# Weights and conditioning loads in separate rings: a two-layer decoder trunk with adaLN

## The chip, the cores and the metric

One Trainium2 chip, one core of it, one program launch. The engines of the core run side by side, each its own queue of instructions: TensorE (PE) with its weight loads (PEld), VectorE (DVE), ScalarE (ACT), GpSimd (POOL), and SyncE (SP), which here only issues transfers from HBM. The metric is the device time of one execution in microseconds; lower is better.

## The reference

Everything is float32; one sequence of 256 positions, model width 1024, two layers.

```python
def ada_mod(c, w, b):
    m = jax.nn.silu(c) @ w + b            # c: (1, 1024), w: (1024, 6144)
    return jnp.split(m[:, None, :], 6, axis=-1)

for layer in range(2):
    shift_m, scale_m, gate_m, shift_f, scale_f, gate_f = ada_mod(c, ada_w[layer], ada_b[layer])
    h = rms_norm(x, norm_gains[layer, 0]) * (1 + scale_m) + shift_m
    y = attn_hybrid_mixer(h, ...) if layer == 0 else retention_mixer(h, ...)
    x = x + gate_m * y
    h = rms_norm(x, norm_gains[layer, 1]) * (1 + scale_f) + shift_f
    gt, up = jnp.split(h @ w_gate_up, 2, axis=-1)       # 2 x 2816 columns
    x = x + gate_f * ((jax.nn.silu(gt) * up) @ w_down)
return rms_norm(x, final_norm)
```

The attention of layer 0 (8 stick-breaking heads, 8 block-sparse heads with rotary) and the retention of layer 1 (4 heads) are small beside the projections: q/k/v 1024x3072, o 1024x1024, retention 1024x6144 and 2048x1024. The six vectors of a layer are one product of a single row with a 1024x6144 matrix, 25 MB a layer, and are all that uses `ada_w`.

## The kernel before, in words

**Weight units.** A float32 product is made of three products of halves: every operand is split into a high part `h` (a copy in the reduced type `float32r`) and a low part `l` (the rest), and `wh*hh`, `wl*hh` and `wh*hl` (lines 422, 423, 426) add up in one PSUM tile. A weight unit is 512 KB, two blocks of 128 rows by 512 columns. SP loads it into a tile `raw`; ACT writes its `wh` (line 220), DVE its `wl` (line 221), each in two pieces of 128x512; then each of the two token tiles (t = 0 and 1, 128 positions each) takes 6 matmuls from it, so 12 in all. There are 228 units: q/k/v 24 (the first 12 in an opening loop of its own over the 8 blocks `kb` of the contraction), o 8, gate-up of layer 0 44, down 22, retention 48 and 16, gate-up of layer 1 44, down 22. The marks `gu0`, `dn0`, `ret`, `gu1`, `dn1` are the numbers of a stage's first unit.

**Buffers.** `raw` is a ring of `NRAW` = 4 tiles (`rawp`), which grows by ten homes during the feed-forward stages, when tiles of the attention stand idle (`raw_homes(True)`). The pairs `wh`/`wl` are a ring of `WBUFS` = 8. Token tile 0 leads token tile 1 by 3 units up to the o projection and by 5 after it (`LAGS`); a pair is held until tile 1 has used it.

**adaLN.** `ada_w` comes in 96 blocks of 512 KB. The 16 blocks of (layer 0, vectors 0 and 1) go through PE in the opening (`ada0_*`). The other 80 go through `ada_unit`: SP loads a block into the same ring `raw`, and DVE multiplies it by its column of silu(c) and adds it to a sum (line 339, `aacc`). `spread` says at which weight unit a block is loaded and summed, ahead of the unit's own load and split. After the eighth block a task turns the sum into columns (`ada_mod`: line 369, a copy on ACT at line 373, then line 379) or a gate (`ada_gate`: ACT line 352, DVE line 353, PE lines 357 and 358). A task's `yield n` lets n ticks of the matmul loop pass; a unit has two ticks for each token tile.

**Order.** PE runs in the order of the program text. ACT, DVE, POOL and SP are put in order when the program is built, by a scheduler that goes by when an instruction can start and by a priority; only instructions that are "pinned" (`tc.keep_in_program_order`, or `pin` while `strict` is set) keep the order of the text among themselves. `more` prepares units `AHEAD` of the one that token tile 0 is at, as far as pairs are free.

**Opening.** For each token: two sums of squares on ACT (line 226), their root (lines 245 to 251), the scaled token (line 255), its transposes on PE (line 953), and a copy by ACT (`xnT`, line 954); with the scale and shift of line 931 and 933 that gives a block of h (DVE line 942, ACT `hh` line 944, DVE `hl` line 947). The first three units' weights come in halves (line 965), and `first_split` splits them. `warm_up` is n matmuls on a tile of zeros.

## Time and profile before

| | |
|---|---|
| median of 3 runs | 771.63 us (769.98, 771.63, 772.52) |
| the profiled execution | 772.73 us, its span 770.9 us |
| PE, PEld busy | 733.2 us (95%), 583.7 us (76%) |
| DVE, ACT, POOL busy | 558.4 us (72%), 405.0 us (53%), 57.1 us (7%) |
| HBM read | 173.16 MB, mean 227 GB/s over the span |

The span runs from the first to the last instruction, and 1.8 us lie around it. PE is the busiest engine: of the profile's 40 slices it is under 9 tenths in the first, the last and five between (116 to 173, 347 to 366 and 501 to 520 us). DVE, at 72% over the whole span, is at 9 tenths or more in eight slices between 77 and 308 us.

### The profile page before, as it was taken

Reading aid. Unit: us, or ns where it says so; the run is one execution under the profiler, and the core shown is the slowest. Engines: PE = TensorE matmul, PEld = TensorE weight load, DVE = VectorE, ACT = ScalarE, POOL = GpSimd, SP = SyncE. Lnnn points to the kernel's source line nnn. Section 1 sums busy time; section 2 is a strip of 40 time slices with the busy share of each in tenths; the row PEclk is TensorE's granted clock in tenths of the full one; section 3 lists DMA queues with packets and bytes.
Section 4 is the critical chain, followed back from the end, with each engine's and each line's share of the span. In section 5 each row is a group of like instructions: output and inputs, shape, how many; then the busy total and the mean of one; then the engine's idle time right before and its main releaser. Section 6 shows DMA issues by size and latency. Waiting matters only on the chain.

```text
span 770.9 us, 10529 instructions
## 1 busy us (share of the span) xinstructions
PE 733.2 (95%) x3564; PEld 583.7 (76%) x3564; DVE 558.4 (72%) x960; ACT 405.0 (53%) x836; POOL 57.1 (7%) x137
## 2 busy tenths in 40 slices
PE   5999998889999999998999999989999999999996
PEld 2777775667888788787787878767877888888884
DVE  3667998779999599647867768676588666665553
ACT  5348645875655455535545454454575455555531
POOL 1001000110000100010111211202110000000000
PEclk9999999999999999999999999999999999999998
DMA  9977888667999879627564747666847787655301
GB/s 306 364 254 244 278 286 292 194 229 252 369 353 333 290 268 393 241 82 217 180 216 142 222 145 226 217 211 201 281 146 214 224 238 211 209 182 180 127 1 54
DMA packets 114806, 174.91 MB, mean 227 GB/s; under 512 B 7496, under 2 KB 71184, under 8 KB 114752
## 3 DMA queue, kind: packets, MB, share of 16 engines
q1 hardware_dynamic: 113376, 171.86, 68.7%
q10 hardware_dynamic: 816, 1.60, 0.6%
q0 software_dynamic: 560, 0.77, 0.3%
q8 instruction: 28, 0.46, 0.3%
q14 instruction: 26, 0.21, 0.1%
HBM read 173.16 MB, written 1.05 MB: 226 GB/s over the span
## 4 chain that ended last, share of the span: by engine, by line
PE 71%; DMA 10%; DVE 8%; ACT 4%; issue 3%; POOL 2%; SPq 0%; DVEq 0%; ACTq 0%; POOLq 0%
PE acc L422 22%; PE acc L426 22%; PE acc L423 21%; DMA raw<-in_ada_w_dram 5%; DVE wl L221 3%; DMA raw<-in_att_w_qkv_dram 2%; DMA raw<-in_att_w_o_dram 2%; ACT wh L220 2%; DVE aacc L339 1%; PE pt L795 1%; DMA early<-in_ada_w_dram 1%; DMA raw<-in_ffn_w_gate_up_dram 1%; PE pt L916 1%; POOL v L248 1%; ACT w L286 1%
## 5 line engine op out<-in xcount | busy, mean ns | idle before, releaser
L221 DVE TENSOR_TENSOR wl<-raw,wh 128x512 fp32r<-128x512 f32 x456 | 297.6, 686 | 123.5 <-ACT wh L220 121.1
L220 ACT ACTIVATE wh<-raw 128x512 fp32r<-128x512 f32 x456 | 265.3, 624 | 208.7 <-PE acc L426 101.4
L422 PE MATMUL acc<-wh,hh 128*128 128x512 f32 x640 | 258.7, 404 | 8.6 <-ACT hh L944 6.8
L423 PE MATMUL acc<-wl,hh 128*128 128x512 f32 x640 | 251.0, 392 | 0.0
L426 PE MATMUL acc<-wh,hl 128*128 128x512 f32 x640 | 205.4, 396 | 0.8 <-DVE hl L290 0.8
L422 PEld LDWEIGHTS acc<-wh,hh 128*128 128x128 f32 x640 | 120.9, 189 | 36.6 <-ACT hh L944 7.6
L426 PEld LDWEIGHTS acc<-wh,hl 128*128 128x128 f32 x640 | 119.6, 189 | 27.8 <-DVE hl L290 2.0
L423 PEld LDWEIGHTS acc<-wl,hh 128*128 128x128 f32 x640 | 121.2, 189 | 23.3 <-issue 0.2
L339 DVE SCALAR_TENSOR_TENSOR aacc<-raw,sc,aacc 128x1024 f32<-128x1024 f32 x80 | 102.4, 1279 | 18.4 <-DMA raw<-in_ada_w_dram 17.2
L422 PE MATMUL acc<-wh,act 128*128 128x512 f32 x240 | 94.1, 392 | 0.0
L423 PE MATMUL acc<-wl,act 128*128 128x512 f32 x240 | 93.5, 389 | 0.0
L426 PE MATMUL acc<-wh,act 128*128 128x512 f32 x240 | 74.3, 391 | 0.0
L422 PEld LDWEIGHTS acc<-wh,act 128*128 128x128 f32 x240 | 45.1, 188 | 10.0 <-ACT wh L220 0.8
L423 PEld LDWEIGHTS acc<-wl,act 128*128 128x128 f32 x240 | 45.1, 188 | 9.2
L426 PEld LDWEIGHTS acc<-wh,act 128*128 128x128 f32 x240 | 44.8, 188 | 9.2
L784 ACT ACTIVATE w<-acc 128x256 f32<-128x256 f32 x44 | 16.9, 384 | 28.7 <-PE acc L426 28.7
L785 DVE TENSOR_TENSOR w<-w,acc 128x256 f32<-128x256 f32 x44 | 18.3, 416 | 9.9 <-ACT w L784 9.7
L226 ACT ACTIVATE w<-x 128x512 f32<-128x512 f32 x20 | 12.5, 623 | 19.1 <-DVE x L308 18.3
L334 POOL MEMSET aacc<- 128x1024 f32 x10 | 9.4, 960 | 176.9 <-PE pt L369 86.7
L229 POOL TENSOR_SCALAR ss<-ss 128x1 f32<-128x1 f32 x8 | 2.4, 303 | 266.8 <-ACT w L226 266.8
L740 ACT ACTIVATE w<-w,ry 128x512 f32<-128x512 f32 x8 | 5.8, 724 | 30.3 <-POOL ry L215 30.3
L306 DVE TENSOR_TENSOR w<-acc,gate 128x512 f32<-128x512 f32 x16 | 11.0, 687 | 13.0 <-PE acc L426 13.0
(165 smaller groups left out, 606.3 us busy)
## 6 DMA issues: line engine op xcount, KB each, us to landing
raw<-in_ffn_w_gate_up_dram SPq DMA_DIRECT2D x176, 256.0 KB, 4.5
raw<-in_ada_w_dram SPq DMA_DIRECT2D x80, 512.0 KB, 5.3
raw<-in_ffn_w_down_dram SPq DMA_DIRECT2D x44, 512.0 KB, 4.3
raw<-in_ret_w_in_dram SPq DMA_DIRECT2D x32, 512.0 KB, 4.3
raw<-in_att_w_qkv_dram SPq DMA_DIRECT2D x21, 512.0 KB, 6.2
early<-in_ada_w_dram SPq DMA_DIRECT2D x16, 512.0 KB, 8.6
raw<-in_ret_w_in_dram SPq DMA_DIRECT2D x32, 256.0 KB, 3.9
raw<-in_ret_w_o_dram SPq DMA_DIRECT2D x16, 512.0 KB, 4.7
```

What stands on the lines that cost most here:

```text
L220: pin(nc.scalar.activation(hi, src, AF.Copy))
L221: pin(nc.vector.tensor_tensor(lo, src, hi, op=ALU.subtract))
L226: pin(nc.scalar.activation(w2(t), xt[t][:, half * 512:(half + 1) * 512], AF.Square, scale=1.0 / 32.0, accum_out=ss))
L248: pin(g.tensor_scalar(v, s1, s0, None, op0=ALU.add))
L306: nc.vector.tensor_mul(m, ps, gate[:, half * 512:(half + 1) * 512])
L334: nc.gpsimd.memset(a, 0.0)
L339: nc.vector.scalar_tensor_tensor(a, r, sc[:, kk:kk + 1], a, op0=ALU.mult, op1=ALU.add)
L422: nc.tensor.matmul(ps, hi[:, kb, :], a, start=first, stop=False)
L423: nc.tensor.matmul(ps, hi[:, kb, :], b, start=False, stop=False)
L426: nc.tensor.matmul(ps, lo[:, kb, :], wh[:, j * 512:(j + 1) * 512], start=False, stop=last)
L784: nc.scalar.activation(s[:, :256], ps[:, :256], AF.Silu)
L785: nc.vector.tensor_mul(s[:, :256], s[:, :256], ps[:, 256:])
```

## The change

The ring `raw` is left to the weights alone, with three tiles instead of four, and the adaLN blocks get a ring of their own, `ada`, of three. `ada_load` issues a block's load; its sum (`ada_unit`) is written two units later (`LATER`, `step`, `due`), or earlier if three are due, and is pinned on DVE. Weights are loaded `DEPTH` units ahead of their split (`load_upto`): two, or five in the feed-forward stages. The pairs `wh`/`wl` go from 8 to 7. The gate's sum is made in the gate's own tile. In the tasks, `GW` goes from 6 to 12 ticks and the two waits of `ada_mod` from 4 and 3 to 6 and 6.

Of the first gate (layer 0, vector 2) six of eight blocks are loaded in the opening, at `kb` 4 to 7, together with the first three units of the attention stage; the 18 blocks left of 24 are spread over units `first` to `gu0` - 6 instead of `first` + 4 to `gu0` - 4. During the opening, raw tiles also live in the attention's `prob` and `sps` tiles.

In the opening's text, the columns and warm-up now stand inside token 0's start, token 0's transposes behind the scale and shift of block 0, and token 1's whole start behind the first splits of all three units; two more matmuls on zeros stand ahead of token 1's transposes.

```diff
@@ -37,15 +37,17 @@
 GY = 4
 R0, R1, R2 = 6, 4, 14
 QR, QP = 6, 3
-GW = 6
+GW = 12
 PRIO = 600
-WBUFS = 8
+WBUFS = 7
 NPS = 8
-NRAW = 4
+NRAW, NADA = 3, 3
+DEPTH = (2, 5)
+LATER = 2
 WIDE = 2
 CONSTS = 4
 EARLY = 2
-WARM = (5, 1)
+WARM = (5, 1, 2)
 
 
 @with_exitstack
@@ -59,7 +61,7 @@
     nc = tc.nc
 
     cp = ctx.enter_context(tc.tile_pool(name="cp", bufs=1))
-    rawp = ctx.enter_context(tc.tile_pool(name="rawp", bufs=NRAW))
+    rawp = ctx.enter_context(tc.tile_pool(name="rawp", bufs=1))
     whp = ctx.enter_context(tc.tile_pool(name="whp", bufs=WBUFS))
     hp = ctx.enter_context(tc.tile_pool(name="hp", bufs=1))
     ap = ctx.enter_context(tc.tile_pool(name="ap", bufs=1))
@@ -320,23 +322,41 @@
         homes.append(homes.pop(0))
         return pool.tile([P, 1024], F32, tag=tag, name=nm("raw"), bufs=bufs)
 
-    def raw_homes(wide):
-
-        homes[:] = [(rawp, "raw", NRAW)] * NRAW
-        if wide:
-            homes.extend([(hp, "oqh", 1), (hp, "oql", 1), (wp, "prob", 2), (wp, "sps", 2),
-                          (wp, "prob", 2), (wp, "sps", 2)])
-
-    def ada_unit(l, m, kk):
+    def raw_homes(*more):
+
+        homes[:] = [(rawp, "raw", NRAW)] * NRAW + list(more)
+
+    due = []
+    now = [0]
+
+    def ada_load(l, m, kk):
+        if len(due) == NADA:
+            ada_sums(1)
+        r = rawp.tile([P, D], F32, tag="ada", name=nm("raw"), bufs=NADA)
+        nc.sync.dma_start(r, ada_w[l, kk * P:(kk + 1) * P, m * D:(m + 1) * D])
+        due.append((now[0], (l, m, kk, r)))
+
+    def ada_sums(n):
+
+        for _ in range(n):
+            ada_unit(*due.pop(0)[1])
+
+    def step():
+        now[0] += 1
+        ada_sums(sum(at + LATER <= now[0] for at, _ in due))
+
+    def ada_unit(l, m, kk, r):
         if kk == 0:
-            a = wp.tile([P, D], F32, tag="aacc", name=nm("aacc"), bufs=2)
+            if m in (2, 5):
+                a = cp.tile([P, D], F32, tag="gate", name=nm("gate"), bufs=1)
+            else:
+                a = wp.tile([P, D], F32, tag="aacc", name=nm("aacc"), bufs=2)
             ada_acc[l, m] = a
             nc.gpsimd.memset(a, 0.0)
             nc.gpsimd.dma_start(a[0:1, :], ada_b[l:l + 1, m * D:(m + 1) * D])
         a = ada_acc[l, m]
-        r = raw_tile()
-        nc.sync.dma_start(r, ada_w[l, kk * P:(kk + 1) * P, m * D:(m + 1) * D])
-        nc.vector.scalar_tensor_tensor(a, r, sc[:, kk:kk + 1], a, op0=ALU.mult, op1=ALU.add)
+        tc.keep_in_program_order(nc.vector.scalar_tensor_tensor(
+            a, r, sc[:, kk:kk + 1], a, op0=ALU.mult, op1=ALU.add))
         if kk == KD - 1:
             if m in (2, 5):
                 spawn(ada_gate(l, m))
@@ -344,8 +364,7 @@
                 spawn(ada_mod(l, m - 1))
 
     def ada_gate(l, m):
-        a = ada_acc.pop((l, m))
-        g = cp.tile([P, D], F32, tag="gate", name=nm("gate"), bufs=1)
+        a = g = ada_acc.pop((l, m))
         for i in range(2):
             c = slice(i * 512, (i + 1) * 512)
             hi, lo = (wp.tile([P, 512], F32R, tag="w2", name=nm("gh"), bufs=2) for _ in range(2))
@@ -362,7 +381,7 @@
 
     def ada_mod(l, m):
         accs = [ada_acc.pop((l, m)), ada_acc.pop((l, m + 1))]
-        yield 4
+        yield 6
         yield ("ps", 1, 1)
         p = pt()
         for g in range(4):
@@ -372,7 +391,7 @@
         r = w2()
         nc.scalar.activation(r, p, AF.Copy)
         release(1)
-        yield 3
+        yield 6
         yield ("ps", 1, 1)
         p = pt()
         for j in range(4):
@@ -394,9 +413,9 @@
 
     def load(i):
         if i == marks["gu0"] + WIDE or i == marks["gu1"] + WIDE:
-            raw_homes(True)
+            raw_homes((hp, "oqh", 1), (hp, "oql", 1), *idle)
         elif i == marks["ret"]:
-            raw_homes(False)
+            raw_homes()
         src, _ = units[i]
         raw = raw_tile().rearrange("p (k f) -> p k f", k=2)
         if isinstance(src, list):
@@ -934,7 +953,7 @@
 
     def ada0_block(kb, rr, ts=(0, 1)):
         k1 = slice(kb, kb + 1)
-        if 0 in ts:
+        if rr is not None:
             ada0_mods(kb, rr)
         hs = {}
         for t in ts:
@@ -958,7 +977,8 @@
         pin(scaled(xns[t][i], xt[t][:, i * 512:(i + 1) * 512], rstd[t]))
 
     NP = KD // 2
-    raw_homes(False)
+    idle = [(wp, tag, 2) for _ in range(2) for tag in ("prob", "sps")]
+    raw_homes(*idle)
     raws = [raw_tile() for g in range(3)]
     for j in range(2):
         for g in range(3):
@@ -971,6 +991,9 @@
     def token_start(t):
         for i in range(2):
             square(t, i)
+        if t == 0:
+            columns()
+            warm_up(WARM[1])
         rstd.append(rms_rstd(t, nc.vector))
         xns.append([w2(t), w2(t)])
         xnT.append(wp.tile([P, KD, P], F32, tag="aacc", name=nm("xnT"), bufs=2))
@@ -984,17 +1007,16 @@
     strict[0] = True
     log_table()
     token_start(0)
-    columns()
-    warm_up(WARM[1])
-    xn_T(0, 0)
     rr = ada0_sum(rows.pop(0))
     gain_columns()
     ws = [w_tiles() for g in range(3)]
     first_split(0, 0)
-    token_start(1)
-    ada0_block(0, rr, (0,))
+    ada0_mods(0, rr)
+    xn_T(0, 0)
+    ada0_block(0, None, (0,))
     first_split(1, 0)
     first_split(2, 0)
+    token_start(1)
     strict[0] = False
 
     def next_loads(kb):
@@ -1002,8 +1024,23 @@
             wraw.append([load(g * NP + kb // 2 + 1) for g in range(3)])
         if kb in (0, 2):
             rows.append(ada0_load(kb // 2 + 3))
-        elif kb + 1 == KD:
+        step()
+        if kb == KD - 2:
+            raw_homes()
+            load_upto(first + NRAW)
+        for q in {4: (0, 1), 5: (2,), 6: (3, 4), 7: (5,)}.get(kb, ()):
+            ada_load(0, 2, q)
+        if kb + 1 == KD:
             att_alloc()
+
+    first = 3 * NP
+    raw_units = {}
+    loaded = [first]
+
+    def load_upto(j):
+        while loaded[0] < min(j, len(units)):
+            raw_units[loaded[0]] = load(loaded[0])
+            loaded[0] += 1
 
     wraw = []
     for kb in range(KD):
@@ -1019,9 +1056,10 @@
             if kb == g == 0:
                 for i in range(3):
                     units[i * NP][1](0, *ws[i], js=(0,))
+                warm_up(WARM[2])
+                strict[0] = True
                 xn_T(1, 0)
-                strict[0] = True
-                ada0_block(0, rr, (1,))
+                ada0_block(0, None, (1,))
                 strict[0] = False
                 rr = ada0_sum(rows.pop(0))
             for t in range(0 if kb else 1, NT):
@@ -1038,18 +1076,17 @@
                 first_split(g, 1)
             if kb == CONSTS and g == 2:
                 att_consts()
-    first = 3 * NP
 
 
     ada_at = {}
 
     def spread(lm, lo, hi):
-        seq = [(l, m, q) for l, m in lm for q in range(KD)]
+        seq = [(l, m, q) for l, m in lm for q in range(6 if (l, m) == (0, 2) else 0, KD)]
         for j, e in enumerate(seq):
             pos = lo + (hi - lo) * j // len(seq)
             ada_at.setdefault(pos, []).append(e)
 
-    spread([(0, 2), (0, 3), (0, 4)], first + 4, marks["gu0"] - 4)
+    spread([(0, 2), (0, 3), (0, 4)], first, marks["gu0"] - 6)
     spread([(0, 5), (1, 0), (1, 1), (1, 3), (1, 4)], marks["gu0"] + 6, marks["ret"] - 8)
     spread([(1, 2)], marks["ret"] + 6, marks["gu1"] - 8)
     spread([(1, 5)], marks["gu1"] + 6, marks["dn1"])
@@ -1063,9 +1100,12 @@
     def more(upto):
         while ready[0] < min(upto, n):
             i = ready[0]
+            load_upto(i + 1 + DEPTH[marks["gu0"] + WIDE <= i < marks["ret"] - DEPTH[1] or
+                                    i >= marks["gu1"] + WIDE])
+            wts[i] = prep(raw_units.pop(i))
+            step()
             for e in ada_at.get(i, ()):
-                ada_unit(*e)
-            wts[i] = prep(load(i))
+                ada_load(*e)
             ready[0] += 1
 
     def go(t):
```

Each fence below gives the instructions in the order of one engine's queue, of before and of the change; line numbers are those of the kernel in question (the split's lines 220 and 221 are 222 and 223 after, the sum's 339 is 358). A name before the arrow is what is written.

On ACT in the opening, before, from token 1's sums of squares on (`raw_113`, `raw_114`, `raw_115` are the first three weight units, `x_87` is token 1, `hh_151` is token 0's h):

```order
L220 ACTIVATE wh_189<-raw_113 128x512
L226 ACTIVATE w_1_38_198,ss_197<-x_87 128x512
L226 ACTIVATE w_1_40_202,ss_201<-x_87 128x512
L245 ACTIVATE ry_204<-ss_201,ss_197 128x1
L246 ACTIVATE ry_204<-ry_204 128x1
L220 ACTIVATE wh_189<-raw_113 128x512
L220 ACTIVATE wh_191<-raw_114 128x512
L944 ACTIVATE hh_151<-w_0_50_223 128x128
```

The same place on ACT now (`hh_157` is token 0's h, `xnT_156` its transposed tile):

```order
L222 ACTIVATE wh_183<-raw_113 128x512
L973 ACTIVATE xnT_156<-pt_196 128x512
L963 ACTIVATE hh_157<-w_0_38_202 128x128
L222 ACTIVATE wh_185<-raw_114 128x512
L222 ACTIVATE wh_187<-raw_115 128x512
L228 ACTIVATE w_1_40_211,ss_210<-x_87 128x512
L228 ACTIVATE w_1_42_215,ss_214<-x_87 128x512
L222 ACTIVATE wh_183<-raw_113 128x512
L247 ACTIVATE ry_217<-ss_214,ss_210 128x1
```

Token 0's h has moved ahead of token 1's root and of the second half of the first unit's split; token 1's root has moved behind two further splits.

On SP in the attention stage, before, where weight loads (line 406) and adaLN loads (line 338) take their tiles from one ring:

```order
L406 DMA raw_806<-in_att_w_qkv_dram 128x2x512
L338 DMA raw_865<-in_ada_w_dram 128x1024
L338 DMA raw_868<-in_ada_w_dram 128x1024
L406 DMA raw_871<-in_att_w_qkv_dram 128x2x512
L338 DMA raw_898<-in_ada_w_dram 128x1024
L338 DMA raw_901<-in_ada_w_dram 128x1024
L406 DMA raw_904<-in_att_w_qkv_dram 128x2x512
```

A piece of the same stage on SP now (weights at line 425, adaLN at line 336), the two from rings of their own:

```order
L425 DMA raw_847<-in_att_w_qkv_dram 128x2x512
L336 DMA raw_856<-in_ada_w_dram 128x1024
L425 DMA raw_909<-in_att_w_qkv_dram 128x2x512
L425 DMA raw_948<-in_att_w_qkv_dram 128x2x512
L336 DMA raw_919<-in_ada_w_dram 128x1024
L336 DMA raw_957<-in_ada_w_dram 128x1024
L425 DMA raw_1002<-in_att_w_qkv_dram 128x2x512
L336 DMA raw_1011<-in_ada_w_dram 128x1024
```

The two kinds still share the one queue, but weight loads stand further forward, and there is about one adaLN load to a weight load instead of two.

On DVE in the second half of the retention, before (`bs` and `mv` are a head's group-norm statistics, `wl` the weights' low parts, `aacc_5664` the sum of layer 1's second gate, line 508 the first step of a rotary embedding):

```order
L221 TENSOR_TENSOR wl_4858<-raw_4855,wh_4857 128x512
L339 SCALAR_TENSOR_TENSOR aacc_5664<-raw_5667,sc,aacc_5664 128x1024
L221 TENSOR_TENSOR wl_4858<-raw_4855,wh_4857 128x512
L731 BN_STATS bs_4799<-pt_4792 128x6
L732 BN_AGGR mv_4800<-bs_4799 128x2
L734 SCALAR_TENSOR_TENSOR w_1_1010_4803<-pt_4792,mv_4800,sg_4484 128x512
L221 TENSOR_TENSOR wl_4885<-raw_4882,wh_4884 128x512 x2
L221 TENSOR_TENSOR wl_4916<-raw_4913,wh_4915 128x512 x2
L339 SCALAR_TENSOR_TENSOR aacc_3657<-raw_4991,sc,aacc_3657 128x1024
L508 TENSOR_TENSOR w_1_1027_4877<-acc_4767,rrope_3521 128x512
```

The same place on DVE now:

```order
L223 TENSOR_TENSOR wl_4840<-raw_4738,wh_4839 128x512 x2
L750 BN_STATS bs_4804<-pt_4797 128x6
L751 BN_AGGR mv_4805<-bs_4804 128x2
L753 SCALAR_TENSOR_TENSOR w_1_1011_4808<-pt_4797,mv_4805,sg_4488 128x512
L223 TENSOR_TENSOR wl_4862<-raw_4785,wh_4861 128x512 x2
L223 TENSOR_TENSOR wl_4889<-raw_4837,wh_4888 128x512 x2
L358 SCALAR_TENSOR_TENSOR gate_3718<-raw_4845,sc,gate_3718 128x1024
L527 TENSOR_TENSOR w_1_1028_4881<-acc_4772,rrope_3528 128x512
```

The sum of the later gate no longer stands among the statistics; the retention's own gate sum still stands ahead of the rotary step.

On DVE at the start of the retention, before (`x_86` is token 0, line 255 its two scaled halves):

```order
L308 TENSOR_TENSOR x_86<-x_86,w_0_695_3427 128x512
L221 TENSOR_TENSOR wl_3574<-raw_3570,wh_3573 128x512 x2
L221 TENSOR_TENSOR wl_3588<-raw_3585,wh_3587 128x512
L339 SCALAR_TENSOR_TENSOR aacc_3657<-raw_3660,sc,aacc_3657 128x1024
L255 TENSOR_SCALAR w_0_707_3449<-x_86,ry_3441,ra_3446 128x512
L255 TENSOR_SCALAR w_0_708_3451<-x_86,ry_3441,ra_3446 128x512
```

And now:

```order
L310 TENSOR_TENSOR x_86<-x_86,w_0_696_3434 128x512
L223 TENSOR_TENSOR wl_3565<-raw_3419,wh_3564 128x512 x2
L223 TENSOR_TENSOR wl_3579<-raw_3546,wh_3578 128x512 x2
L257 TENSOR_SCALAR w_0_708_3456<-x_86,ry_3448,ra_3453 128x512
L257 TENSOR_SCALAR w_0_709_3458<-x_86,ry_3448,ra_3453 128x512
```

The sum that stood ahead of token 0's scaling is gone from there.

## Rows read from the trace of the kernel before

**Rows 1.** Windows: us, PE (count), PEld, DVE, ACT, POOL busy, PEclk, DMA, GB/s

```profile
60.00:140.00 80.00, 74.42 (x426) 54.46 (x425) 68.68 (x96) 48.64 (x100) 5.51 (x8) 1.00 0.84 280
140.00:160.00 20.00, 17.50 (x105) 14.56 (x104) 15.68 (x35) 15.44 (x41) 1.74 (x4) 0.91 0.60 179
180.00:260.00 80.00, 80.00 (x366) 65.69 (x365) 74.70 (x112) 43.23 (x88) 1.51 (x2) 1.00 1.00 340
500.00:520.00 20.00, 17.02 (x76) 13.93 (x75) 13.72 (x22) 10.93 (x20) 1.20 (x5) 0.91 0.70 214
```

**Rows 2.** Timeline of the opening, 11 to 25 us: start, us, instruction, [idle before]

```profile
11.08 0.62 ACT L226 ACTIVATE w<-x 128x512 f32<-128x512 f32 x1
...
14.14 0.15 DVE L933 TENSOR_TENSOR sm<-pt,gains 128x1 f32<-128x1 f32 x1
...
16.27 1.31 ACT L220 ACTIVATE wh<-raw 128x512 fp32r<-128x512 f32 x2 [3.25 <-DMA raw<-in_att_w_qkv_dram]
...
17.54 0.34 DVE L942 TENSOR_SCALAR w<-xnT,gm,sm 128x128 f32<-128x128 f32 x1
...
18.27 0.79 PE L422 MATMUL acc<-wh,hh 128*128 128x512 f32 x1 [6.08 <-ACT hh L944]
...
23.18 0.60 ACT L954 ACTIVATE xnT<-pt 128x512 f32<-128x512 f32 x1 [3.40 <-PE pt L953]
...
24.55 0.50 PE L422 MATMUL acc<-wh,hh 128*128 128x512 f32 x1 [0.40 <-ACT hh L944]
```

**Rows 3.** Waits of 60 to 180 us: us in total, times, longest

```profile
PE pt L379 <- ACT w L373: 2.5, 1, 2.5
...
PE pt L488 <- DVE w L515: 2.1, 1, 2.1
...
PE acc L422 <- ACT hh L285: 1.8, 2, 1.4
...
PE pt L643 <- DVE rc L631: 1.5, 1, 1.5
...
PE pt L595 <- DVE sps L587: 1.0, 1, 1.0
...
PE pt L593 <- DVE sps L587: 0.8, 1, 0.8
```

**Rows 4.** Groups of 60 to 146 us: count, busy, mean ns, idle before

```profile
L339 DVE SCALAR_TENSOR_TENSOR aacc<-raw,sc,aacc 128x1024 f32<-128x1024 f32 x24 | 30.7, 1280 | 3.4 <-DMA raw<-in_ada_w_dram 2.4 <-DMA aacc<-in_ada_b_dram 0.7
...
L220 ACT ACTIVATE wh<-raw 128x512 fp32r<-128x512 f32 x35 | 20.6, 630 | 19.2 <-DMA raw<-in_att_w_qkv_dram 10.4 <-DMA raw<-in_att_w_o_dram 8.7
```

**Rows 5.** Waits of SP's queue, 60 to 146 us

```profile
SPq L406 <- DVE aacc L339: 14.7, 12, 3.3
```

**Rows 6.** Timeline of 358 to 362 us, start of the retention

```profile
358.77 0.19 POOL L251 TENSOR_SCALAR ra<-ra 128x1 f32<-128x1 f32 x1
359.42 1.28 DVE L339 SCALAR_TENSOR_TENSOR aacc<-raw,sc,aacc 128x1024 f32<-128x1024 f32 x1 [1.33 <-DMA raw<-in_ada_w_dram]
360.62 1.00 DVE L255 TENSOR_SCALAR w<-x,ry,ra 128x512 f32<-128x512 f32 x2
```

**Rows 7.** Waits of 500 to 540 us

```profile
PE pt L488 <- DVE w L515: 3.0, 1, 3.0
...
PE pt L357 <- ACT gh L352: 1.0, 1, 1.0
```

**Rows 8.** Chain that ended last, 480 to 512 us: start, us, what

```profile
487.67 6.52 DMA raw<-in_ada_w_dram
494.28 1.28 DVE aacc L339
...
508.03 1.09 PE pt L488 x4
```

**Rows 9.** Transfers of 40 to 60 us: GB/s in 40 slices of 0.5 us

```profile
GB/s 346 348 346 346 358 354 377 381 385 381 393 393 385 414 344 369 367 375 213 78 49 29 0 0 0 61 143 307 381 156 0 0 66 74 279 389 275 70 127 262
```

**Rows 10.** Groups of 180 to 260 us

```profile
L220 ACT ACTIVATE wh<-raw 128x512 fp32r<-128x512 f32 x56 | 33.0, 626 | 28.6 <-PE acc L426 20.1 <-issue 7.5 <-DMA raw<-in_ffn_w_gate_up_dram 1.0
```

## The prediction, made before the changed kernel had run

> **What bounds the kernel now.** The windows come first. From 180 to 260 us PE is busy 80.00 of 80 us at a granted clock of 1.00 [rows 1]: where the projections run undisturbed, PE's matmuls set the time, and nothing around them can shorten it. The change adds and removes no product of a weight; it can only give back time in which PE stands still or runs at a lower clock. So I went through the waits that end on PE, window by window, and made four pools of them.
>
> The opening, by the timeline: PE's first matmul with a weight starts at 18.27 after 6.08 us of waiting for token 0's h [rows 2]. The scale and shift that h needs were ready at 14.14 + 0.15 = 14.29, but DVE took h up at 17.54. In between the first unit's second half had to be copied on ACT, which had waited 3.25 us for its transfer. Token 1's first matmul comes at 24.55.
>
> Attention, 60 to 146 us: PE waits 2.5 + 2.1 + 1.5 + 1.0 + 0.8 = 7.9 us, for ACT's copy in `ada_mod` (line 373) and for DVE (lines 515, 587 and 631) [rows 3]. From 140 to 160 the granted clock is 0.91 [rows 1], so some of PE's work ran at 1.2 instead of 2.4 GHz; 20 us x 0.09 = 1.8 us. Together 9.7. DVE is busy 68.68 of 80 us before that [rows 1], and 24 adaLN sums of 1280 ns are 30.7 us of it [rows 4]. ACT stands idle 19.2 us before the weights' copies, all but 0.1 us of it for weight transfers [rows 4], and SP's weight loads wait 14.7 us, in 12 waits, for an adaLN sum to free a `raw` tile [rows 5]. Thus weights come late because DVE sums late, and DVE works in bursts. After that, at the o projection's end and the norm behind it, PE waits 1.8 us (line 285) [rows 3].
>
> Start of the retention: the root for token 0 is ready at 358.77 + 0.19 = 358.96, but DVE sits in an adaLN sum whose block came late, and scales the token from 360.62: 1.66 us [rows 6].
>
> Late retention: PE waits 3.0 us for the rotary step (line 515) and 1.0 for the gate (line 352) [rows 7], and the clock is 0.91 from 500 to 520 [rows 1], again 1.8 us; together 5.8. The chain of waits goes back through DVE to an adaLN block that took 6.52 us to land and to its sum of 1.28 us [rows 8].
>
> **The change part by part.** The sum is made against the profiled execution, 772.73 us.
>
> Opening order: in ACT's new order token 0's h stands ahead of the late half, and so it does on DVE. Its earliest start is 14.29 instead of 17.54, so 3.25 us is the most to be had; nothing is the least, if the next wait (token 1) only grows. Token 1's first matmul tells: now its two sums of squares (0.62 us each [rows 2]), a further split, its root and scaling stand behind the splits of units two and three. From h at 14.29 I count h 0.34 and its copy, two splits of 0.65 (half of 1.31), two squares of 0.62, a third split of 0.65, some 1.5 us of small steps on ACT and DVE: 20.3 or so; then its transposes, the copy of 0.60, and h: about 22.5, against 24.55. I take **-2.0** (0 to -3.25).
>
> Attention: three edits work here. The longer waits of `ada_mod` (6 and 6 ticks) go at the 2.5 us for line 373. Six of the 24 sums, 6 x 1.28 = 7.7 us of DVE, move to the opening. And weights in their own ring no longer wait for sums, so the 14.7 us on SP's queue go; in the order, weight loads stand further forward. The blocks that move need room there: from 49 to 60 us the transfers run at some 140 GB/s instead of 350 to 390 [rows 9], so 11 us x 230 GB/s = 2.5 MB are free, for five of the six 0.5 MB blocks. Of the pool of 9.7 us I take **-6**. At least -1.5, since the line 373 wait alone shrinks; at most -9.7. What stays is DVE's own chain: the softmax steps of lines 587 and 631 don't depend on loads.
>
> o projection and norm: 1.8 us hang on ACT and DVE steps of the norm itself; fewer sums in the way give **-0.5** (0 to -1.8).
>
> Start of the retention: the sum is gone from ahead of the scaling in the order, and 1.66 us with it, **-1.6**. A split that is not ready could take its place (0 at worst).
>
> Late retention: the second gate's sum is gone from among the statistics, so its late block no longer holds DVE; the gate's matmuls come 12 ticks after its split instead of 6, which covers the 1.0 us. One sum of 1.28 us still stands ahead of the rotary step. The pool is 3.0 + 1.0 + 1.8 = 5.8, less that 1.28: **-4.5** (-1.0 to -5.8).
>
> New costs: two warm-up matmuls at no more than the 0.79 us that the first product of the opening took [rows 2] are 1.6 us if nothing hides them, but they stand where PE has to wait for token 1's scaling; the pinned sums hold what stands behind them on DVE, 1.28 us each if a block is late; SP's one queue still lets a load that finds no free tile hold the others. I take **+1.0** for all of it (0 to +20, next part).
>
> Seven pairs instead of eight: a split has to wait for PE to free a pair one unit sooner. From 180 to 260 ACT is idle 20.1 us for PE's line 426 before its copies [rows 10], which is slack: copies wait for PE, not PE for copies. So I cost this at nothing; the cover is the time from split to use. PE spends 12 matmuls on a unit; 80 us for the 28 units of those 56 copies are 2.86 us a unit. Eight pairs with a lead of five leave three units, 8.6 us; seven leave two, 5.7 us. A unit needs two copies of 0.63 and two subtractions of about as much on DVE, with at times a sum of 1.28 between: under 4 us.
>
> The sum: -2.0 - 6 - 0.5 - 1.6 - 4.5 + 1.0 = -13.6, so 759.1. The median of before lies 1.1 below its profiled execution (771.63 and 772.73), so **758.0** for a median.
>
> **The rivals.**
>
> *DVE stays the pace of attention* (0.22). The waits for lines 515, 587 and 631 are DVE's own work [rows 3], and DVE is busy 86% there [rows 1]; sums held back by two units and pinned could stand in front of them as well as before. Against it: a quarter of the sums leave. Only 1.5 of the 9.7 and nothing at the norm come back: -2.0 - 1.5 - 1.6 - 4.5 + 1.0 = -8.6, or 763.0.
>
> *All pools come back* (0.13). Then -3.25 - 9.7 - 1.8 - 1.6 - 5.8 + 1.0 = -21.2: 750.5. For it speaks that each wait names a cause that the change touches; against it the sum ahead of the rotary step, and that PE's waits in attention have four causes.
>
> *Too few pairs: slower* (0.08). Where a unit's splits finish later than PE needs them, each unit of the feed-forward and retention stages waits. There are 196 from `gu0` on. Without its cost the change gives 14.6, so a wait of 14.6 / 196 = 0.075 us a unit eats all; at 0.1 us it is 19.6 - 14.6 = +5.0, or 776.6. Against it: the 20.1 us of slack on ACT [rows 10]. For it: DVE has only 5.3 us of 80 free from 180 to 260 [rows 1], so it can't catch up once it is late, and the three `raw` tiles of the retention hold fewer loads.
>
> A rule speaks for this rival: the Trainium skill ("Perfetto Trace Analysis", Optimization Strategy) says that the same gap, repeated on the engine that ought to be saturated, can mean too few buffers for the next tile. By that rule fewer pairs invite such gaps, and the time would be the 776.6 above; the trace of before shows the gaps on ACT and none on PE in that stretch, so with eight pairs there is no such shortage, and no run here shows seven yet.
>
> *It does nothing much* (0.09). The scheduler may already issue each load as soon as a tile is free, and the opening's gain may be lost to transfers, which run at 350 to 390 GB/s until 49 us whatever PE does [rows 9]. Then only the start of the retention is left, less the costs: -1.6 + 1.0, or 771.0. Against it: SP's 14.7 us are waits for tiles, not for transfers [rows 5].
>
> **How the numbers follow.** The forecast has 0.48. The lower end, 749.5, takes in the case of all pools; the upper, with the bounds 0, -1.5, 0, -1.6 and -1.0 and the cost, is -3.1: 768.5, and I put it at 768.0. That leaves out the last two rivals, 0.17, and little else. 0.3% (2.3 us) is about what a measurement of this kernel tells from no change. Faster: 0.48 + 0.22 + 0.13 = 0.83; the same: 0.09; slower: 0.08.
>
> **What would show it.** In the changed profile: token 0's first matmul near 15 us and token 1's near 22.5; no wait over 1 us for `ada_mod`'s copy; ACT's idle time for weight transfers in attention well under 19.2 us, and SP's weight loads waiting for no sum; the granted clock 1.00 from 140 to 160 and from 500 to 520; the scaling at the retention's start right behind the root; PE still at 80 of 80 in a stretch of gate-up of layer 0. The prediction is wrong if PE waits for `wh` or `wl` in many units of the feed-forward stages, if new PE waits stand where the sums went (50 to 60 us), or if DVE's softmax steps come as late as before.

## The result

The changed kernel took 761.24 us, the median of 4 runs (760.49 to 761.71), beside 772.08 for the kernel before in the same session: a ratio of 0.9855, interval [0.9834, 0.9876]. That is about 1.4% faster (by the interval 1.2 to 1.7%), inside the predicted range, 3.2 us above the predicted 758.0 and 1.8 below the 763.0 of the first rival. The profiled execution has a span of 759.9 us against 770.9.

The windows of the changed kernel (us, then PE, PEld, DVE, ACT, POOL busy with counts, granted clock, DMA share, GB/s), to be read beside [rows 1]:

```profile
60.00:80.00 20.00, 17.18 (x79) 12.15 (x77) 14.52 (x19) 15.90 (x30) 2.83 (x4) 0.83 0.69 221
80.00:120.00 40.00, 40.00 (x227) 29.83 (x225) 38.70 (x52) 24.37 (x47) 0.00 (x0) 1.00 0.89 306
140.00:160.00 20.00, 18.62 (x119) 15.31 (x116) 12.70 (x26) 13.40 (x35) 3.54 (x7) 1.00 0.55 171
180.00:260.00 80.00, 80.00 (x367) 65.62 (x366) 71.46 (x108) 43.27 (x88) 0.00 (x0) 1.00 0.98 323
490.00:510.00 20.00, 19.61 (x93) 16.04 (x93) 13.37 (x22) 10.70 (x21) 2.14 (x7) 1.00 0.71 228
500.00:520.00 20.00, 20.00 (x92) 16.36 (x91) 13.00 (x23) 10.28 (x20) 4.53 (x10) 1.00 0.72 230
```

From 180 to 260 nothing has changed for PE, with seven pairs too. The work that lay from 500 to 520 before, 17.02 us at 0.91, now lies some 8 us earlier (the rotary step at 499.69 instead of 508.03): from 490 to 510 PE is busy 19.61 us at a full clock. But from 60 to 80 there is a new low clock of 0.83 (20 x 0.17 = 3.4 us of PE's work) and a new wait. The waits that end on PE from 60 to 180 us (total, times, longest), beside [rows 3]:

```profile
PE acc L441 <- ACT wh L222: 2.8, 1, 2.8
...
PE pt L662 <- DVE rc L650: 1.5, 2, 1.2
...
PE pt L552 <- ACT prob L665: 0.6, 1, 0.6
PE pt L662 <- DVE w L651: 0.6, 1, 0.6
PE acc L445 <- DVE hl L292: 0.6, 1, 0.6
PE pt L279 <- DVE w L257: 0.6, 1, 0.6
...
PE acc L441 <- ACT hh L287: 0.5, 1, 0.5
```

The modulation's wait of 2.5 us and the rotary step's of 2.1 are gone, and so are the two for `sps` (1.0 and 0.8); the wait for `rc` is still 1.5 us. The first line is new: PE waits for a weight's copy. ACT's timeline shows where the copy was (start, us, instruction):

```profile
68.41 0.62 ACT L222 ACTIVATE wh<-raw 128x512 fp32r<-128x512 f32 x1
68.93 1.08 ACT L603 ACTIVATE w<-pt 128x512 f32<-128x512 f32 x2
69.89 1.16 ACT L604 ACTIVATE w<-w 128x512 f32<-128x512 f32 x2
70.93 1.15 ACT L605 ACTIVATE w<-w 128x512 f32<-128x512 f32 x2
71.97 0.60 ACT L872 ACTIVATE att_v<-acc 128x512 f32<-128x512 f32 x1
72.44 1.68 ACT L222 ACTIVATE wh<-raw 128x512 fp32r<-128x512 f32 x3
```

Between the two halves of one unit's copy (68.41 and 72.44) ACT works through the absolute values, exponentials and logarithms of the stick-breaking heads (lines 603 to 605) and a copy of v, and PE stands.

The opening, beside [rows 2]: token 0's first product at 14.19 instead of 18.27, token 1's at 21.96 instead of 24.55.

```profile
14.19 0.80 PE L441 MATMUL acc<-wh,hh 128*128 128x512 f32 x1 [1.41 <-ACT hh L963]
...
19.24 0.55 DVE L257 TENSOR_SCALAR w<-x,ry,ra 128x512 f32<-128x512 f32 x1
20.59 0.60 ACT L973 ACTIVATE xnT<-pt 128x512 f32<-128x512 f32 x1 [2.35 <-PE pt L972]
...
21.96 0.50 PE L441 MATMUL acc<-wh,hh 128*128 128x512 f32 x1 [0.40 <-ACT hh L963]
```

And the start of the retention, beside [rows 6]: the scaling now follows the root at once.

```profile
355.76 0.19 POOL L253 TENSOR_SCALAR ra<-ra 128x1 f32<-128x1 f32 x1
355.99 1.00 DVE L257 TENSOR_SCALAR w<-x,ry,ra 128x512 f32<-128x512 f32 x2 [0.53 <-POOL ra L253]
```

**Where the 11.0 us of span came from.** Five points of PE's timeline can be found in both kernels, and in all that follow: the first rotary product of attention, the transposes of token 1's norm ahead of the first feed-forward part and ahead of the retention, those of token 0 ahead of the second feed-forward part, and the end.

| stage | before | changed | gain | predicted |
|---|---|---|---|---|
| to the first rotary product | 64.33 | 62.41 | 1.9 | 2.0 |
| attention, o, norm | 109.05 (to 173.38) | 107.53 (to 169.94) | 1.5 | 6 + 0.5 |
| gate-up, down, norm | 196.73 (to 370.11) | 195.20 (to 365.14) | 1.5 | 1.6 |
| retention, norm | 202.04 (to 572.15) | 195.86 (to 561.00) | 6.2 | 4.5 |
| the rest | 198.75 (to 770.9) | 198.9 (to 759.9) | -0.15 | |

The forecast also had 1.0 of new costs. So attention gave 5 us less than forecast, and the retention 1.7 more.

### The profile page after: what moved, and what is told of

It reads as the page before. It is cut to its first block, busy times and chain, and to the rows that moved or that the text cites. A ratio compares the mean times of both kernels' runs of the same rounds, so it can differ in the third digit from the quotient of the medians.

```text
span 759.9 us, 10517 instructions
## 1 busy us (share of the span) xinstructions
PE 735.6 (97%) x3568; PEld 583.3 (77%) x3568; DVE 557.7 (73%) x960; ACT 404.1 (53%) x836; POOL 55.8 (7%) x137
## 4 chain that ended last, share of the span: by engine, by line
PE 66%; DVE 5%; ACT 2%; issue 2%; POOL 1%; DMA 1%; DVEq 0%; SPq 0%; ACTq 0%; POOLq 0%
PE acc L445 21%; PE acc L441 21%; PE acc L442 20%; DVE wl L223 2%; PE pt L814 1%; ACT wh L222 1%; PE pt L730 1%; DMA raw<-in_ret_w_in_dram 1%; DVE w L257 0%; PE pt L747 0%; PE pt L279 0%; PE pt L507 0%; DVE w L529 0%; DVE gate L358 0%; DVE w L534 0%
## 5 line engine op out<-in xcount | busy, mean ns | idle before, releaser
L358 DVE SCALAR_TENSOR_TENSOR aacc<-raw,sc,aacc 128x1024 f32<-128x1024 f32 x48 | 61.3, 1278 | 0.8 <-DMA raw<-in_ada_w_dram 0.8
L358 DVE SCALAR_TENSOR_TENSOR gate<-raw,sc,gate 128x1024 f32<-128x1024 f32 x32 | 40.9, 1279 | 0.1
L228 ACT ACTIVATE w<-x 128x512 f32<-128x512 f32 x20 | 12.5, 624 | 16.4 <-DVE x L310 15.8
```

What stands on the lines that cost most here:

```text
L228: pin(nc.scalar.activation(w2(t), xt[t][:, half * 512:(half + 1) * 512], AF.Square, scale=1.0 / 32.0, accum_out=ss))
L358: tc.keep_in_program_order(nc.vector.scalar_tensor_tensor(a, r, sc[:, kk:kk + 1], a, op0=ALU.mult, op1=ALU.add))
```

## The experiments

They were run in three sessions (e1 to e4, e5 to e8, e9 to e12), each beside the kernel before, whose medians there were 770.66, 770.64 and 770.39 us; the changed kernel was not run in them again. So the table gives each kernel's ratio to the kernel before of its own session. It also gives two stages of the profiled execution as above: from the first rotary product (A) to token 1's first feed-forward norm (B), and from B to the end. These are from one execution of each kernel. Behind B, kernels with the same pairs and ticks agree within 0.7 us; how far A to B differs between executions of one kernel no trace shows, and the whole time of the kernel before went from 766.82 to 776.74 us over 29 runs. Differences of a few us from A to B are therefore held against the medians.

| kernel | median us | ratio, interval | A | A to B | B to end |
|---|---|---|---|---|---|
| before | | | 64.33 | 109.05 | 597.5 |
| changed | 761.24 | 0.9855 [0.9834, 0.9876] | 62.41 | 107.53 | 590.0 |
| e1 weights first | 762.89 | 0.9902 [0.9878, 0.9926] | 64.81 | 105.48 | 590.2 |
| e2 gate spread | 763.68 | 0.9916 [0.9892, 0.9940] | 62.22 | 108.22 | 590.7 |
| e3 opening alone | 771.91 | 1.0024 [1.0003, 1.0045] | 62.08 | 110.77 | 597.9 |
| e4 short ticks | 767.08 | 0.9955 [0.9932, 0.9978] | 62.24 | 111.86 | 593.3 |
| e5 sums cut | 757.73 | 0.9829 [0.9806, 0.9852] | 62.50 | 103.10 | 590.4 |
| e6 sums on GpSimd | 802.40 | 1.0406 [1.0381, 1.0432] | 62.80 | 147.84 | 590.3 |
| e7 old opening | 762.41 | 0.9885 [0.9860, 0.9909] | 63.68 | 107.51 | 590.1 |
| e8 before, seven pairs | 765.89 | 0.9938 [0.9912, 0.9963] | 63.76 | 108.03 | 592.3 |
| e9 before, pairs, ticks | 768.35 | 0.9963 [0.9940, 0.9986] | 64.53 | 110.64 | 590.2 |
| e10 before, ticks | 773.28 | 1.0026 [1.0003, 1.0048] | 63.95 | 110.19 | 597.3 |
| e11 before, pairs, ticks, opening | 768.67 | 0.9971 [0.9949, 0.9993] | 62.41 | 114.42 | 590.7 |
| e12 changed, six pairs | 780.49 | 1.0116 [1.0079, 1.0153] | 62.29 | 104.80 | 609.9 |

**e1: weights ahead of the gate's blocks.** In `next_loads`:

```diff
+        if kb == 4:
+            raw_homes()
+            load_upto(first + 2)
         if kb == KD - 2:
-            raw_homes()
             load_upto(first + NRAW)
```

> The changed kernel, but the first two weight units of the attention stage are loaded at block 4 of the opening, ahead of the gate's blocks, instead of at block 6 behind three of them. My theory: the new wait of 2.8 us at 69.8 us and the granted clock of 0.83 from 60 to 80 us (20 x 0.17 = 3.4 us) come from these loads standing late in the queue: ACT's order puts the split's second half of the second unit behind the stick-breaking exponentials. Then this kernel loses that wait, has a clock of 1.00 from 60 to 80, and takes 755 to 757 us against 761.2. Rival: DVE and ACT are full there in any case, the wait moves to another line within 60 to 100 us, and the time stays within 760 to 762.

The wait at 69.8 us was gone, and the clock was 1.00 from 60 to 80; so late loads had put that copy behind the exponentials. A to B became 2.1 us shorter. But the time did not fall; 762.89 lies just above the rival's range. PE now waits 2.2 us at the end of the opening (A at 64.81), and behind A its longest wait is 2.7 us, for ACT's exponentials of the block-sparse heads (line 647), with a clock of 0.91 from 120 to 140. Its timeline shows the wait at the end of the opening:

```profile
55.52 3.69 DVE L223 TENSOR_TENSOR wl<-raw,wh 128x512 fp32r<-128x512 f32 x6
...
59.14 2.74 DVE L358 SCALAR_TENSOR_TENSOR gate<-raw,sc,gate 128x1024 f32<-128x1024 f32 x2
62.11 0.60 DVE L961 TENSOR_SCALAR w<-xnT,gm,sm 128x128 f32<-128x128 f32 x2
62.49 0.56 ACT L963 ACTIVATE hh<-w 128x128 fp32r<-128x128 f32 x2 [4.93 <-DVE w L961]
...
62.85 0.50 PE L441 MATMUL acc<-wh,hh 128*128 128x512 f32 x1 [2.21 <-ACT hh L963]
```

Two pinned gate sums stand on DVE ahead of the last block of h. They stand there in the changed kernel too, but 2.3 us earlier, where PE does not wait for them:

```profile
55.60 1.28 DVE L223 TENSOR_TENSOR wl<-raw,wh 128x512 fp32r<-128x512 f32 x2
56.80 2.60 DVE L358 SCALAR_TENSOR_TENSOR gate<-raw,sc,gate 128x1024 f32<-128x1024 f32 x2
```

What is new in e1 is that six subtractions instead of two stand in front of them, since the weights come earlier. The first half of my theory held (what the wait came from), the second (that 5 us would come back) fell.

**e2: no gate blocks in the opening.** The line with `{4: (0, 1), 5: (2,), ...}` is left out, and `spread` takes all eight blocks.

> The changed kernel without the six gate blocks in the opening: all eight are loaded in the attention stage, 24 blocks over the same 14 units. My theory of late weight loads: the wait at 69.8 us goes (up to 6 us back), but six sums more, 7.7 us of DVE, come into the stage, and PE waits for DVE in it again; 757 to 763 us. Rival, that the moved sums are worth what the prediction said (most of 6 us) and the wait has nothing to do with them: 765 to 768 us.

763.68 lies between the two ranges. The wait at 69.8 went, and others came (the longest 1.9 us, again for line 647). A to B became 0.7 us longer, and by the medians the kernel is 2.4 us slower than the changed one; the intervals of the ratios don't overlap. Two things change at once here, so the price of the six sums alone is not shown. Against e1, where that wait is gone as well, A to B is 2.7 us longer and the median 0.8 us higher, which is little beside the 7.7 us of DVE that the prediction counted for them.

**e3 and e7: the opening by itself, and the change without it.** e3 is the kernel before with the hunks of `token_start`, `ada0_block`, the opening's text and `WARM`; e7 the changed kernel with those hunks undone.

> The kernel before with the opening's new order alone (token 1's start behind the three splits, two more warm-up matmuls), nothing else changed. My theory: token 1's first matmul comes at about 22 us instead of 24.55 and what is won there is carried to the end: 769.4 to 770.2 us against 772.1 (ratio 0.9965 to 0.9975). Rival: transfers and splits of the attention stage take it back, 771.5 to 772.5 us.

> The changed kernel with the old order of the opening (token 1's start ahead of token 0's h, one warm-up matmul less a place). By the theory that DVE's work paces the attention stage, the 2.6 us that token 1's first matmul comes later (24.55 instead of 21.96) are lost up to the stage and taken back in it: 760.5 to 762.5 us. Rival, that the opening's gain is carried to the end: 763 to 764.5 us.

e3 reached A 2.25 us earlier and B 0.5 earlier, and its time is not below that of before: the rival held. In e7 the old opening reaches A 1.3 us later, and that stays to B: 762.41 lies in the range of the theory, but nothing was taken back in the stage, as the theory had it. The interval overlaps that of the changed kernel. Alone the new opening is worth nothing; within the change it is about 1 us, which is not clear of noise.

**e4: the old ticks.** `GW` = 6, and `yield 4` and `yield 3` in `ada_mod`.

> The changed kernel with the tasks' old waits: 6 ticks for a gate, 4 and 3 for the modulation, instead of 12, 6 and 6. My theory: the wait of 2.5 us for the modulation's copy in attention and the 1.0 us for the late gate come back in part, 762.5 to 765 us. Rival: with the sums pinned and earlier these waits are covered anyway, and the time stays at 760.5 to 762 us.

It lost more than I expected: 4.3 us from A to B, 3.3 behind B (the profiled execution lies 2 us above the kernel's median, so the first number is a high one).

**e5: most of the attention's sums left out.**

```diff
+        cols = 8 if l == 0 and (m in (3, 4) or m == 2 and kk > 5) else D
         tc.keep_in_program_order(nc.vector.scalar_tensor_tensor(
-            a, r, sc[:, kk:kk + 1], a, op0=ALU.mult, op1=ALU.add))
+            a[:, :cols], r[:, :cols], sc[:, kk:kk + 1], a[:, :cols], op0=ALU.mult, op1=ALU.add))
```

> The changed kernel with work left out: the 18 adaLN sums of the attention stage treat 8 of their 1024 columns, so the vectors come out wrong; loads, queue order and everything else stay. It takes some 18 x 1.2 = 21 us of work from DVE. In the runs so far the first layer's norm came at 161.0 to 161.2 us whether the attention stage began at 62.2, 62.4 or 64.8 us. My new theory: DVE's total work paces that stage. Then the norm comes at 152 to 155 us and the kernel takes 752 to 755 us. Rival: PE's waits there are the latency of the softmax's own chain over ACT and DVE, whatever else DVE does; then 759 to 762 us.

DVE from 80 to 120 us fell from 38.70 to 27.40 of 40, and A to B became 4.4 us shorter, 103.10. Neither theory's numbers came out: 757.73 lies between the two ranges. Some 20 us less work on DVE gave back 4.4 us at most. From 80 to 120 PE had been at 40.00 of 40 already, so nothing was to be had there; from 120 to 140 it rose from 18.44 to 20.00 of 20. The wait of 2.8 us from 60 to 80 stayed, with a clock of 0.91 instead of 0.83, which is up to 1.6 of the 4.4. By the ratios e5 is 0.3% faster than the changed kernel, and the intervals overlap. So DVE's load paces a part of the stage at most.

**e6: those sums on GpSimd.** `nc.gpsimd.tensor_scalar` (the product, in place) and `nc.gpsimd.tensor_tensor` (the addition) for the same 18 blocks.

> The changed kernel with the 18 adaLN sums of the attention stage on GpSimd, as a product and an addition each. If DVE's work paces the stage and GpSimd's work costs DVE nothing, 752 to 756 us. If GpSimd takes over 5 us a block, the vectors come late and it is 765 us or more; if the two slow each other, DVE's instructions get longer in the profile and the time is 758 to 764 us.

5.6 us a block by the means, and DVE slowed as well. Groups of 60 to 160 us (count, busy, mean ns, idle before):

```profile
L223 DVE TENSOR_TENSOR wl<-raw,wh 128x512 fp32r<-128x512 f32 x32 | 31.7, 1023 | 36.5 <-ACT wh L222 36.5
...
L359 POOL TENSOR_SCALAR raw<-raw,sc 128x1024 f32<-128x1024 f32 x16 | 51.7, 3233 | 7.9 <-DMA raw<-in_ada_w_dram 7.5 <-issue 0.4
L360 POOL TENSOR_TENSOR aacc<-aacc,raw 128x1024 f32<-128x1024 f32 x13 | 30.8, 2367 | 1.1
```

In the changed kernel the same subtraction (line 223) has a mean of 692 ns in this window; here it is 1023.

**e8: seven pairs alone.** `WBUFS = 7` in the kernel before.

> The kernel before with seven pairs of wh and wl instead of eight, nothing else changed. My theory: the pairs' cover of two units is enough, 771 to 772.5 us (ratio 0.999 to 1.002). Rival: a price of 0.02 to 0.1 us on each of 196 units, 775 to 791 us.

Neither: 0.6% faster. Behind B it gains 5.2 us, and at the start of the retention its timeline reads as the changed kernel's does, though its sums are not pinned and its ring is shared:

```profile
357.76 0.19 POOL L251 TENSOR_SCALAR ra<-ra 128x1 f32<-128x1 f32 x1
357.98 1.00 DVE L255 TENSOR_SCALAR w<-x,ry,ra 128x512 f32<-128x512 f32 x2 [0.53 <-POOL ra L251]
```

The late sum of [rows 6] has gone from ahead of the scaling with nothing changed but the pairs.

**e9 to e11: the two numbers without the rings.** e9 is the kernel before with `WBUFS` = 7 and the ticks 12, 6, 6; e10 with the ticks alone; e11 is e9 with the new opening.

> The kernel before with two numbers of the change alone: seven pairs instead of eight, and the tasks' waits of 12, 6 and 6 ticks. One ring of four for weights and blocks, sums beside the load and not pinned, the old opening. Seven pairs alone gave 0.9938, and taking the ticks out of the changed kernel cost it about 6 us. My theory now: these two numbers are the change's gain, 760 to 762.5 us (ratio 0.986 to 0.990). Rival: the rings and the pinned, later sums are needed for it, 764 to 767 us.

> The kernel before with the tasks' waits of 12, 6 and 6 ticks alone. They should remove the 2.5 us wait for the modulation's copy and the 1.0 us for the late gate, with what the clock adds: 766 to 769 us if they work by themselves; 770 to 772.5 us if DVE's order, left as it was, takes it back.

> The kernel before with seven pairs, the ticks and the new order of the opening. Alone, and when undone in the changed kernel, the opening moved the end by little. If DVE paces the attention stage, this is 760 to 762.5 us like the same kernel without the opening; if the opening's 2 us are carried over, 758 to 760 us, and the best so far.

Behind B, e9 and e11 equal the changed kernel: 590.2 and 590.7 against 590.0. There pairs and ticks are the whole gain, 7.5 us: 5.2 by the pairs (e8), the rest by the ticks, which alone gave 0.2 (e10). From A to B they read 1.1 to 5.4 us longer than before. All three came out slower than either of their two ranges. e9's PE waits of 60 to 180 us:

```profile
PE acc L422 <- ACT wh L220: 4.1, 2, 2.1
PE pt L643 <- DVE rc L631: 1.4, 1, 1.4
...
PE acc L423 <- DVE wl L221: 1.2, 2, 0.7
```

PE waits for splits in attention, and the clock is 0.83 from 120 to 140. e11 differs from the changed kernel by the rings, the earlier loads, the pinned and later sums and where the blocks stand (six of them in the opening, the gate's sum in the gate's tile). It takes 114.42 us from A to B against 107.53, and its median is 7.4 us higher. So those are worth 6.9 us there, given the rest; my theory that two numbers were the gain fell.

**e12: six pairs.** `WBUFS = 6` in the changed kernel.

> The changed kernel with six pairs. A lead of five units leaves one unit, 2.9 us, between a pair's release and its use, and two copies and two subtractions with a sum between take up to 4 us: PE waits for splits in the feed-forward stages, 0.1 us a unit or more over some 196 units: 780 us or more. Rival: fewer pairs only bring the critical chain's work forward on ACT and DVE, as from eight to seven: 757 to 762 us.

780 us or more was the number, but the cover ends in another place than I said. From 180 to 260 us PE is still at 80.00 of 80; the loss is in the retention (215.84 us from norm to norm, 195.86 with seven), where PE's waits of 365 to 577 us begin with:

```profile
PE acc L441 <- ACT wh L222: 10.7, 8, 1.9
PE acc L442 <- DVE wl L223: 4.1, 10, 2.2
```

From A to B six pairs read 2.7 us shorter than seven, in an execution 1.7 us below the kernel's median.

## Why the prediction was right, and where not

**Size and sign.** -13.6 was forecast, the spans moved by -11.0. Two terms were off, in opposite directions: attention gave 5 us less than forecast, the retention 1.7 more, and that they partly cancel in the sum is luck. What was forecast behind B came, but by pairs and ticks and not by the rings. The first rival's 763.0 lies nearer to 761.24 than the forecast's 758.0; the range held both.

**Attention, -6: the step that failed.** It said that SP's 14.7 us of waits go, since weights in their own ring no longer wait for sums. That row is gone, but the waiting is not. SP's queue from 60 to 146 us, first two more rows of before, to be read beside [rows 5], then the changed kernel:

```profile
SPq L338 <- DVE wl L221: 20.2, 11, 4.1
SPq L338 <- DVE aacc L339: 10.1, 9, 1.8
```

```profile
SPq L425 <- DVE wl L223: 25.9, 14, 5.0
SPq L336 <- DVE aacc L358: 15.2, 13, 2.0
SPq L336 <- DVE gate L358: 10.1, 6, 4.1
```

Now a weight load waits for the subtraction that frees its tile, 25.9 us in 14 waits, and the adaLN loads, which stand in the same queue, wait 25.3 us for sums. All waits of this queue for DVE add up to 61.7 us before and 61.3 now; the prediction had looked at one row of them. ACT's idle time for weight transfers, forecast to fall well under 19.2 us [rows 4], is 18.0:

```profile
L222 ACT ACTIVATE wh<-raw 128x512 fp32r<-128x512 f32 x40 | 23.4, 630 | 18.0 <-DMA raw<-in_att_w_o_dram 13.0 <-DMA raw<-in_att_w_qkv_dram 5.0
```

Most of the old waits of PE did go: from 80 to 120 us PE is at 40.00 of 40, and the clock is 1.00 from 140 to 160. But the copy behind the exponentials took 2.8 us, and the clock after it up to 3.4. The pool of 9.7 us that the forecast drew on holds 9.2 again: 5.8 of waits up to 146 us and those 3.4. Over 60 to 180 us PE's waits fell from 10.5 to 7.4 us while the clock's loss rose from 1.8 to 3.4, which leaves the 1.5 of the table. e1 shows that late loads caused the new wait, and that taking them away uncovers the next ones. The first rival, that DVE keeps pacing the stage (-1.5), had the size of this term right; its reason holds in part, since taking some 20 us of sums off DVE gives 4.4 us at most (e5).

**Six sums moved, 7.7 us of DVE.** What their move alone is worth was not measured: with them back in the stage, A to B is 0.7 us longer than in the changed kernel and 2.7 longer than in e1 (e2). In the opening they are not always free: in e1 two of them hold up the last block of h.

**Opening, -2.0.** Measured 1.9 at A, with token 1 at 21.96 against my count of about 22.5. What lies behind it was not asked: alone it is lost by B (e3), in the change about 1.3 us stay (e7).

**Start of the retention, -1.6: right size, and the sum is gone from ahead of the scaling.** The stage gave 1.5. But the rings don't get the credit: e8 shows the same rows by seven pairs alone.

**Late retention, -4.5.** 6.2 with the norm behind it. The 3.0 and 1.0 us waits and the low clock are gone. I had left 1.28 us for the sum ahead of the rotary step; that sum still stands there (DVE has it at 495.86, the rotary step at 497.06), and PE waits 0.4 us at 499.69. The stage from norm to norm takes 202.04 us before, 197.76 with seven pairs alone (e8), 201.93 with the ticks alone (e10), 195.88 with both (e9) and 195.86 in the changed kernel; so the credit goes to pairs and ticks. The forecast's reason, a late sum gone from among the statistics, is not needed for it. In e8 a sum still stands among them, and none stands right ahead of the rotary step; the next one comes behind it:

```profile
490.82 0.69 DVE L731 BATCH_NORM_STATS2 bs<-pt 128x6 f32<-128x512 f32 x1
491.43 1.27 DVE L339 SCALAR_TENSOR_TENSOR aacc<-raw,sc,aacc 128x1024 f32<-128x1024 f32 x1
...
499.85 0.69 DVE L508 TENSOR_TENSOR w<-acc,rrope 128x512 f32<-128x512 f32 x1
...
503.89 1.28 DVE L339 SCALAR_TENSOR_TENSOR aacc<-raw,sc,aacc 128x1024 f32<-128x1024 f32 x1 [0.35 <-DMA raw<-in_ada_w_dram]
```

PE's longest wait for the rotary step is 0.4 us there too. The gate's 1.0 us is the part that the ticks cover, as forecast: it stays in e8 and is gone in e9.

**Seven pairs, costed at nothing.** The cover held, with PE at 80.00 of 80. But fewer pairs do more than hold less: alone they gained 0.6%, where the forecast had nothing. That the order on DVE is then another is shown at the retention's start; why it came out better, and whether the next kernel would have the same luck, is not. The Trainium skill's rule ("Perfetto Trace Analysis", Optimization Strategy) on too few buffers did not bite at seven; at six it did, in the retention, with 14.8 us of PE waits for splits.

What stays open: which of rings, earlier loads, pinned sums and the blocks' places gives the 6.9 us between e11 and the changed kernel. Of these only the six blocks of the opening were tried (e2). Six pairs in attention with seven behind it was not tried either: 62.29 + 104.80 of e12 and 590.0 of the changed kernel would be a span of 757.1, an estimate from single executions.

## What to carry to other kernels

Where two engines' orders are made by a scheduler, the number of buffers is also an order: run the kernel with that one number changed before crediting the restructuring around it (here seven pairs alone took 5 of 11 us, and six lost 19). Don't add up the waits of a stage in which several engines take turns at holding PE: a wait removed can uncover the next, here on DVE and on ACT (e1, e2), and a gain ahead of the stage can be lost in it (e3), though in the changed kernel 1.3 us of it stayed (e7). Parts of such a change don't add: the ticks alone were worth nothing (e10), within the change some 6 us by the medians (e4).

## What the runs showed of the hardware

GpSimd's product of 128x1024 float32 by a column took 3.2 us and the addition 2.4, where DVE does both in one instruction of 1.28; and DVE's subtraction went from 692 to 1023 ns beside them (e6). The Trainium skill ("GPSIMD Engine Reference", Specifications) says that GpSimd shares its SBUF interface with VectorE and contends with instructions of two SBUF inputs; the subtraction has two, and this trace agrees. DVE's `sps` step, which reads one of its two inputs from PSUM, kept its 685 ns (line 610 in e6, 606 in the changed kernel).

The granted clock of a window fell with single waits: 0.83 from 60 to 80 with a wait of 2.8 us in the changed kernel. The same wait of 2.8 us went with 0.91 in e4, e5 and e12, so what one wait costs in clock differed by a factor of two. In e6, whose longest wait was 12.5 us, the windows of 60 to 180 are at 0.95 down to 0.66.
